# A decoder layer on one core: row sums and the residual's scale and shift move to VectorE beside the index search, and the search is spread over more products

## The chip, the cores and the metric

The kernel runs on one core of a Trainium2 chip. A core has five engines, each with its own queue of instructions that it works through in order: TensorE (PE; its weight loads are listed as PEld), VectorE (DVE), ScalarE (ACT), GpSimd (POOL) and SyncE (SP), which here only issues DMA transfers. They wait for each other through semaphores. The metric is the device time of one execution in microseconds (us), the median of several runs.

## The reference

The reference computes one decoder layer for 512 tokens of width 1024, in float32. Cut to what matters here:

```python
h = layer_norm(x, ln_emb_g, ln_emb_b)
q_att, c_kv, q_idx, k_idx, w_idx, cv_b, cv_c, cv_x, g_att, g_conv = split(h @ w_in)
score = sum over 8 heads of relu(q_idx . k_idx / 8) * w_idx        # 512 x 512, causal
sel   = the 128 best keys of each query's row
att   = softmax(q . k over sel) . values                            # 8 heads, latent rank 128
conv_y = cv_b * causal_dwconv3(cv_c * cv_x)
merged = sigmoid(g_att + b0) * (att @ w_br_att) + sigmoid(g_conv + b1) * (conv_y @ w_br_conv)
h = layer_norm(ALPHA * h + merged @ w_o, ln1_g, ln1_b)              # ALPHA = 2 ** 0.25
# then a gated MLP with a causal width-3 convolution, an embedding term and a last layer_norm
```

## The kernel before

Everything is kept in float32 accuracy by splitting each operand of a product into a high part and a low part (the rest): a product is three matmuls, high by high, high by low and low by high (L157 to L159). For each chunk of weights (128x1024 numbers) SP loads the raw numbers (wr), ACT casts the high part (wh, L76), and DVE or POOL subtracts to get the low part (wl, L143). A letter of the chunk, "v" or "p", says which of the two.

The program is a list of steps, one or two chunks each, and each engine's queue simply gets its instructions in the order in which the code is written: nothing reorders them. `plan()` builds the steps. Ahead of step i come the casts and low parts of chunks some steps ahead (`advance`, with a lead of 3 steps and 4 raw buffers), then the functions that are entered for that step in `preps`, then the step itself. The order of the steps is: the index queries (q_idx) with the scores between them, two early products of the convolution, then from `at_first` on conv block 0's b, the four attention queries (qa, split by POOL), the c, x and b products of conv blocks 1 to 3, then gates (gt, and gtb by blocks), branches (br), the output product (wo) and the MLP.

Three streams of side work stand between these steps.

- **The index search.** For each of three blocks of 128 queries (over 256, 384 and 512 keys), 16 rounds on DVE find the best eight scores of each row (MAX8, L596) and strike them out (MATCH_REPLACE8, L598). A last operation (madd, L601) makes the mask. The scores themselves are summed on DVE (L586). The search is a generator: behind each step, the run loop takes rounds until their summed costs, an estimate that the generator gives for each, pass a budget, SIDE_NS. Each round is put down at 2.084 times the number of keys plus 395, in ns: 928, 1195 and 1462.
- **The attention.** Its steps are tied to later steps of the list (ATT_AT). One step sends the logits (lg) through a reduction on DVE with the mask (L671), exponentials on ACT (L675), a reciprocal and the scaling on DVE (L677, L679); a later one transposes the rows on PE (pT, L687). A step that needs a mask which is not ready takes the rest of that block's rounds first. The third block of queries (384 keys) is the first to go in two halves.
- **The conv blocks.** For each, DVE multiplies c and x (cvu, L764), ACT and POOL apply the three taps (cvt, L750 to L755), DVE multiplies by b (cvy, L771), and ACT and POOL split the result (cvT, L773 and L774).

The residual: x's normalized rows (`xb`, before the embedding norm's scale and shift) are spilled to DRAM at the end of `start()`, loaded again as `hr` when memory is free, and multiplied by ALPHA times the scale (ge) and shifted by ALPHA times the shift (be) there (L1028, L1029), ahead of the last branches. ACT makes the two ALPHA products (L1024), and `onto` puts the rows into the accumulators of wo (L1047).

The row sums: four sums and differences of blocks of the transposed h (`hx` in the trace, `first_sum`, L795), needed for the gates by blocks, run on POOL in the four steps from `at_first` − 1 on; their splits (fsh, fsl) come nine steps later and more.

Of the kernel before, what the change touches and what calls it, by code (L numbers as in the profile page):

```python
# [11 lines left out]
OP = mybir.AluOpType  # L12
# [3 lines left out]
D = 1024  # L16
NB = S // P
# [7 lines left out]
ALPHA = 2.0 ** 0.25  # L25
# [60 lines left out]
class Kern:  # L86
# [1 line left out]
    WHL = 4  # L88
    LEAD = 3
    NK4 = 28  # L90
    SIDE_NS = 3600
    ATT_AT = (-2, 0, 3, 5, 7, 9, 12, 14)

    def __init__(self, ctx, tc, a, out):
# [60 lines left out]
    def mm3(self, out, wh, wl, xh, xl, start, stop):  # L155
        t = self.nc.tensor
        t.matmul(out, wh, xh, start=start, stop=False)  # L157
        t.matmul(out, wh, xl, start=False, stop=False)  # L158
        t.matmul(out, wl, xh, start=False, stop=stop)  # L159
# [105 lines left out]
    def start(self):  # L265
        nc, a = self.nc, self.a
# [217 lines left out]
        rest = small_norm((2, 3))  # L484
        self.advance(0, 5)
        rest()
        for b in range(NB):
            nc.sync.dma_start(self.hdram[b], self.xb[b])
        for i in range(3):
            nc.sync.dma_start(self.pwdram[i], pw[i].rearrange("p b n -> p (b n)"))  # L490

# [20 lines left out]
    def plan(self):  # L512
        nc, a = self.nc, self.a
# [276 lines left out]
        def first_sum(n):  # L790

            b11, b12, b21, b22 = (self.hblock[g, h] for g in range(2) for h in range(2))
            to, x, y, op = ((b11, b11, b12, OP.subtract), (b12, b22, b12, OP.subtract),
                            (b22, b11, b22, OP.add), (b21, b22, b21, OP.subtract))[n]
            return lambda: nc.gpsimd.tensor_tensor(to, x, y, op=op)  # L795

        def first_parts(n):
            def f():
# [10 lines left out]
        def block_mm(o, w, at, rows, start, stop):  # L809
            wh, wl = (t.rearrange("p (k m) -> p k m", k=KC)[:, 4 * at:4 * at + 4] for t in (w.hi, w.lo))  # L810
            for c, (xh, xl) in enumerate(rows):
                for i, (l, r) in enumerate(((wh, xh), (wh, xl), (wl, xh))):
                    nc.tensor.matmul(o, l[:, c], r, start=start and c + i == 0, stop=stop and c == 3 and i == 2,  # L813
                                     skip_group_check=True)
# [147 lines left out]
        at_first = len(self.steps)  # L962
# [7 lines left out]
        at_slot, pairs = [], {}  # L970
# [29 lines left out]
        for n in range(4):  # L1000
            self.preps.setdefault(at_first - 1 + n, []).append(lambda n=n: first_sum(n)())
            self.preps.setdefault(at_first + (9, 11, 12, 13)[n], []).append(first_parts(n))
# [4 lines left out]

        def res_load():

            ge, be = self.k4("ge"), self.k4("be")  # L1010
            self.bcast("ln_emb_g", D, ge, nc.sync)
            self.bcast("ln_emb_b", D, be, nc.sync)
            self.res_affine = ge, be

        def res_rows():
            self.hr = []
# [2 lines left out]
                nc.sync.dma_start(t, self.hdram[b])  # L1019
                self.hr.append(t)  # L1020

        def res_scale():
            for t in self.res_affine:
                nc.scalar.mul(t, t, ALPHA)  # L1024

        def res_affine(b):
            t, (ge, be) = self.hr[b], self.res_affine
            nc.vector.tensor_tensor(t, t, ge, op=OP.mult)  # L1028
            nc.vector.tensor_tensor(t, t, be, op=OP.add)  # L1029

        def ln1_load():
            self.g1, self.b1 = self.k4("g1"), self.k4("b1")
            self.bcast("ln1_g", D, self.g1)
            self.bcast("ln1_b", D, self.b1)

        self.preps.setdefault(at_slot[15], []).append(res_load)
        self.preps.setdefault(at_slot[17], []).append(res_rows)
        self.preps.setdefault(at_slot[19], []).append(res_scale)
        for b in range(NB):
            self.preps.setdefault(at_slot[20 + b // 2], []).append(lambda b=b: res_affine(b))  # L1040

        self.zps = {}

# [423 lines left out]
        for n, (name, i) in enumerate(copies):  # L1467
            at = at_ple - 2 + n // 2 if n < 4 else at_ple + 1 + (n - 4) * 4 // 5 if n < 20 else at_ple + 16 + 3 * (n - 20)
# [224 lines left out]
    def run(self):  # L1693
        for i, fn in enumerate(self.steps):
# [5 lines left out]
            if self.side_from is not None and i >= self.side_from:  # L1700
                left = self.SIDE_NS
                while left > 0:
# [93 lines left out]
```

## Time and profile before

| | before |
|---|---|
| median of 3 runs | 745.28 us (745.15 to 746.37) |
| the profiled execution | 745.23 us |
| its span, first to last instruction | 743.5 us |
| around the span | 1.7 us |
| mean granted clock of PE | 0.991 |
| busy: PE, DVE, ACT, POOL | 725.6, 615.6, 425.6, 269.2 us |

A time at the head of a row of the timeline is counted from the start of the span; the second number is the duration, and a bracket at the end holds the idle time ahead of the row and what ended it. In a row of waits stand the sum, the number of times and the longest. In a group's row stand the busy time and the mean duration in ns of one. Where the first index block ends and so on is told by the shapes: 128x256, 128x384 and 128x512 rows are the search over 256, 384 and 512 keys.

### The profile page before, as it was taken

To read this page: it belongs to the slowest core of one execution; us is meant where nothing else is said; L and a number is where in the kernel's file an instruction comes from. 1 tells how busy PE (TensorE), PEld (TensorE's weight loads), DVE (VectorE), ACT (ScalarE), POOL (GpSimd) and SP (SyncE) were. 2 spreads that over 40 slices of the span, in tenths; PEclk is the share of its full clock that TensorE was granted. 3 is DMA by queue.
4 is the path that set the end of the run, shared out by engine and by line. 5 is a ranking of instruction groups with operands and counts; after the bars stand their busy time and mean duration, and the time that the engine had idled before them with its cause. 6 is when DMAs were issued, how large, how long until landed. Compare 5 with 4: busy or idle time off the path is not lost.

```text
span 743.5 us, 12196 instructions
## 1 busy us (share of the span) xinstructions
PE 725.6 (98%) x4399; PEld 640.4 (86%) x4399; DVE 615.6 (83%) x1045; ACT 425.6 (57%) x718; POOL 269.2 (36%) x332
## 2 busy tenths in 40 slices
PE   9999899999999999799999999999999999999995
PEld 5998678888879998588888999999999998888885
DVE  5867999975557657889898899999999889987797
ACT  5645434468766554343565666777667665665630
POOL 4304698765755821320101233443332212211002
PEclk9999999999999999899999999999999999999999
DMA  9473379759999999195998999899989878999661
GB/s 354 109 274 100 102 255 370 267 185 271 233 218 184 224 274 395 42 314 203 299 393 250 323 276 253 223 250 250 236 233 254 235 216 212 273 256 278 224 212 57
DMA packets 61867, 178.02 MB, mean 239 GB/s; under 512 B 7232, under 2 KB 7360, under 8 KB 61424
## 3 DMA queue, kind: packets, MB, share of 16 engines
q1 hardware_dynamic: 43968, 140.56, 53.8%
q0 software_dynamic: 16976, 35.27, 26.8%
q10 hardware_dynamic: 864, 1.43, 0.6%
q8 instruction: 34, 0.56, 0.3%
q14 instruction: 25, 0.20, 0.1%
HBM read 171.46 MB, written 70.78 MB: 326 GB/s over the span
## 4 chain that ended last, share of the span: by engine, by line
PE 88%; DVE 6%; ACT 2%; POOL 1%; DMA 1%; issue 1%; DVEq 0%; ACTq 0%; POOLq 0%
PE ffb L813 23%; PE gtb L813 5%; PE dn L1527 5%; PE dn L1526 5%; PE dn L1528 5%; PE cv L157 2%; PE cv L159 2%; PE cv L158 2%; PE gt L157 2%; PE wo L918 2%; PE wo L917 2%; PE gt L159 2%; PE gt L158 2%; PE wo L916 2%; PE pg L1168 2%; PE pg L1169 2%
## 5 line engine op out<-in xcount | busy, mean ns | idle before, releaser
L143 DVE TENSOR_TENSOR wl<-wr,wh 128x1024 fp32r<-128x1024 f32 (+1 forms) x175 | 199.8, 1157 | 45.9 <-ACT wh L76 44.5
L76 ACT CAST wh<-wr 128x1024 fp32r<-128x1024 f32 (+1 forms) x186 | 180.5, 978 | 73.3 <-PE dn L1528 15.7
L1453 POOL TENSOR_TENSOR behind<-token,neghalf 128x1 f32<-128x1 f32 x112 | 82.3, 857 | 241.4 <-ACT token L1452 205.2
L813 PE MATMUL ffb<-hsh,wh 128*128 128x256 f32 x304 | 86.1, 283 | 0.0
L813 PE MATMUL ffb<-hsl,wh 128*128 128x256 f32 x304 | 86.0, 283 | 0.0
L813 PE MATMUL ffb<-hsh,wl 128*128 128x256 f32 x304 | 86.0, 283 | 0.0
L813 PE MATMUL ffb<-h1T,wh 128*128 128x256 f32 x456 | 83.9, 283 | 0.1
L813 PEld LDWEIGHTS ffb<-h1T,wh 128*128 128x128 f32 x456 | 71.1, 192 | 0.4 <-ACT c L1368 0.3
L813 PE MATMUL ffb<-h1T,wl 128*128 128x256 f32 x228 | 64.7, 284 | 0.2 <-DVE wl L143 0.2
L813 PEld LDWEIGHTS ffb<-hsl,wh 128*128 128x128 f32 x304 | 58.4, 192 | 0.0
L813 PEld LDWEIGHTS ffb<-hsh,wh 128*128 128x128 f32 x304 | 58.4, 192 | 0.0
L813 PEld LDWEIGHTS ffb<-hsh,wl 128*128 128x128 f32 x304 | 58.4, 192 | 0.0
L143 POOL TENSOR_TENSOR wl<-wr,wh 128x1024 fp32r<-128x1024 f32 x15 | 36.0, 2406 | 27.5 <-ACT wh L76 27.5
L813 PEld LDWEIGHTS ffb<-h1T,wl 128*128 128x128 f32 x228 | 43.7, 192 | 0.4 <-DVE wl L143 0.4
L185 POOL TENSOR_TENSOR rstd<-veps,neghalf 128x1 f32<-128x1 f32 x12 | 8.0, 666 | 99.3 <-DVE nm L208 65.2
L1329 POOL DMA_DIRECT2D ws<-ws x38 | 39.3, 1170 | 11.2 <-issue 6.1
L1329 POOL DMA_DIRECT2D ws<-in_w_a x38 | 36.2, 1363 | 6.1 <-issue 3.9
L159 PE MATMUL cv<-hT,wl 128*128 128x512 f32 x80 | 31.3, 391 | 0.4 <-POOL wl L143 0.4
L157 PE MATMUL cv<-hT,wh 128*128 128x512 f32 x80 | 31.4, 392 | 0.0
L158 PE MATMUL cv<-hT,wh 128*128 128x512 f32 x80 | 31.1, 389 | 0.0
L743 DVE SCALAR_TENSOR_TENSOR ff<-c,vec,ff 128x510 f32<-128x510 f32 x38 | 28.5, 750 | 1.3
L740 ACT ACTIVATE ff<-c,vec 128x512 f32<-128x512 f32 x38 | 29.3, 811 | 0.4 <-DVE c L1374 0.2
(363 smaller groups left out, 2087.8 us busy)
## 6 DMA issues: line engine op xcount, KB each, us to landing
wr<-in_w_a SPq DMA_DIRECT2D x61, 512.0 KB, 4.5
ws<-in_w_a SPq DMA_DIRECT2D x76, 256.0 KB, 6.1
wr<-ws SPq DMA_DIRECT2D x38, 512.0 KB, 6.4
ws<-in_w_a POOLq DMA_DIRECT2D x38, 256.0 KB, 8.6
ws<-ws POOLq DMA_DIRECT2D x38, 256.0 KB, 11.0
wr<-in_w_b SPq DMA_DIRECT2D x15, 512.0 KB, 6.0
wr<-in_w_dn SPq DMA_DIRECT2D x15, 512.0 KB, 6.6
wr<-in_w_a SPq DMA_DIRECT2D x19, 256.0 KB, 6.9
```

The source lines that it names most:

```text
L76: nc.scalar.copy(hi, raw)
L143: (self.nc.vector if eng == "v" else self.nc.gpsimd).tensor_tensor(lo, raw, hi.bitcast(F32), op=OP.subtract)
L157: t.matmul(out, wh, xh, start=start, stop=False)
L158: t.matmul(out, wh, xl, start=False, stop=False)
L159: t.matmul(out, wl, xh, start=False, stop=stop)
L740: nc.scalar.activation(dst, src, AF.Identity, bias=v[:, bcol:bcol + 1], scale=v[:, wcol + 2 * tap:wcol + 2 * tap + 1])
L813: nc.tensor.matmul(o, l[:, c], r, start=start and c + i == 0, stop=stop and c == 3 and i == 2, skip_group_check=True)
L1329: return lambda: nc.gpsimd.dma_start(to, what, accum_op=OP.add, max_dma_last_dim=4096)
L1453: nc.gpsimd.tensor_tensor(self.sm("behind", [P, 1], bufs=2), t, self.neghalf, op=OP.mult)
L1526: nc.tensor.matmul(o, ah, wh[:, i, c], start=first, stop=False, skip_group_check=free)
L1527: nc.tensor.matmul(o, ah, wl[:, i, c], start=False, stop=False, skip_group_check=free)
L1528: nc.tensor.matmul(o, al, wh[:, i, c], start=False, stop=last, skip_group_check=free)
```

## The change

Five things are edited; the products on PE and their order stay the same.

- The four `hx` operations of 128x1024 run on DVE in place of POOL, in the same steps.
- ge and be are loaded at step 2 in place of a late step, and ACT multiplies them by ALPHA one step behind `at_first`.
- The scale and shift (two operations of 128x1024 for each of four blocks of rows) act on x's rows, in the eight steps from `at_first` + 3 on, still on DVE, and no longer on the loaded `hr` rows.
- The spills of x's rows to DRAM follow there, each behind its block's two operations; the loads back stay where they were.
- SIDE_NS is 2800 in place of 3600, so fewer rounds of the search follow a step (three of 256 or 384 keys give 2784 and 3585, two of 512 give 2924).

```diff
-    SIDE_NS = 3600
+    SIDE_NS = 2800
...
-        for b in range(NB):
-            nc.sync.dma_start(self.hdram[b], self.xb[b])
...
-            return lambda: nc.gpsimd.tensor_tensor(to, x, y, op=op)
+            return lambda: nc.vector.tensor_tensor(to, x, y, op=op)
...
+        def res_scale():
+            for t in self.res:
+                nc.scalar.mul(t, t, ALPHA)
+
+        def res_affine(b, i):
+            x = self.xb[b]
+            return lambda: nc.vector.tensor_tensor(x, x, self.res[i], op=(OP.mult, OP.add)[i])
+
+        def res_spill(b):
+            return lambda: nc.sync.dma_start(self.hdram[b], self.xb[b])
...
-        def res_affine(b):
-            t, (ge, be) = self.hr[b], self.res_affine
-            nc.vector.tensor_tensor(t, t, ge, op=OP.mult)
-            nc.vector.tensor_tensor(t, t, be, op=OP.add)
...
-        self.preps.setdefault(at_slot[15], []).append(res_load)
-        self.preps.setdefault(at_slot[17], []).append(res_rows)
-        self.preps.setdefault(at_slot[19], []).append(res_scale)
+        for at, f in ((2, res_load), (at_first + 1, res_scale), (at_slot[17], res_rows)):
+            self.preps.setdefault(at, []).append(f)
         for b in range(NB):
-            self.preps.setdefault(at_slot[20 + b // 2], []).append(lambda b=b: res_affine(b))
+            for i in range(2):
+                self.preps.setdefault(at_first + 3 + 2 * b + i, []).append(res_affine(b, i))
+            self.preps.setdefault(at_first + 6 + 2 * b, []).append(res_spill(b))
```

The line numbers of the changed kernel are smaller by two from L490 on: L764 is L762 there, L671 is L669.

First place, DVE's queue around conv block 2, some steps ahead of the first attention reductions. Before (a MAX and a MATCH_REPLACE are one round; tk are the search's rows):

```order
L764 TENSOR_TENSOR cvu_1548<-cv_1523,cvc_1470 128x512
L596 MAX m_358_1558<-tk_0_1427 128x8
L598 MATCH_REPLACE tk_1_1428<-m_358_1558,tk_0_1427 128x512
L596 MAX m_359_1561<-tk_1_1428 128x8
L598 MATCH_REPLACE tk_0_1427<-m_359_1561,tk_1_1428 128x512
L596 MAX m_360_1564<-tk_0_1427 128x8
L598 MATCH_REPLACE tk_1_1428<-m_360_1564,tk_0_1427 128x512
L771 TENSOR_TENSOR cvy_1602<-cv_1577,cvt_1550 128x512
```

The same place in the change, with the last block of x's rows (x_74):

```order
L1018 TENSOR_TENSOR x_74<-x_74,ge 128x1024
L762 TENSOR_TENSOR cvu_1547<-cv_1522,cvc_1468 128x512
L594 MAX m_354_1557<-tk_0_1502 128x8
L596 MATCH_REPLACE tk_1_1503<-m_354_1557,tk_0_1502 128x512
L594 MAX m_355_1560<-tk_1_1503 128x8
L596 MATCH_REPLACE tk_0_1502<-m_355_1560,tk_1_1503 128x512
L1018 TENSOR_TENSOR x_74<-x_74,be 128x1024
L769 TENSOR_TENSOR cvy_1600<-cv_1575,cvt_1549 128x512
```

A step holds two rounds in place of three and one operation on x's rows more. Counted up to the first reductions, the search over 512 keys has 14 rounds there before and 7 in the change; the 32 rounds over 256 and 384 keys stand ahead of them in both.

Second place, DVE's queue between the scaling of the second attention step's rows (p_1) and the reductions of the third. Before:

```order
L679 TENSOR_SCALAR p_1_1888<-p_1_1888,rs_1887 128x256 x4
L679 TENSOR_SCALAR p_1_1889<-p_1_1889,rs_1887 128x256 x4
L143 TENSOR_TENSOR wl_1945<-wr_1571,wh_1944 128x1024
L143 TENSOR_TENSOR wl_1976<-wr_1642,wh_1975 128x1024
L1450 MEMSET token_1981 128x1
```

In the change:

```order
L677 TENSOR_SCALAR p_1_1887<-p_1_1887,rs_1885 128x256 x4
L143 TENSOR_TENSOR wl_1943<-wr_1567,wh_1942 128x1024
L594 MAX m_397_1973<-tk_0_1502 128x8
L596 MATCH_REPLACE tk_1_1503<-m_397_1973,tk_0_1502 128x512
L594 MAX m_398_1976<-tk_1_1503 128x8
L596 MATCH_REPLACE tk_0_1502<-m_398_1976,tk_1_1503 128x512
L143 TENSOR_TENSOR wl_1980<-wr_1637,wh_1979 128x1024
```

Two rounds follow each low part (wl) there; five rounds and the madd stand between these rows and the third reductions, where none stood before. Four more stand between the first attention step's scaling and the second reductions, where two and the madd stood.

Third place, DVE's queue in the last branches, between two low parts. Before:

```order
L143 TENSOR_TENSOR wl_3513<-wr_3364,wh_3512 128x1024
L1028 TENSOR_TENSOR hr_3297<-hr_3297,ge 128x1024
L1029 TENSOR_TENSOR hr_3297<-hr_3297,be 128x1024
L1028 TENSOR_TENSOR hr_3299<-hr_3299,ge 128x1024
L1029 TENSOR_TENSOR hr_3299<-hr_3299,be 128x1024
L902 TENSOR_TENSOR sig_2740<-br_3522,sig_2740 128x512
```

In the change:

```order
L143 TENSOR_TENSOR wl_3517<-wr_3374,wh_3516 128x1024
L900 TENSOR_TENSOR sig_2754<-br_3522,sig_2754 128x512
L902 TENSOR_TENSOR sig_2754<-sig_2754 128x512
L900 TENSOR_TENSOR sig_2914<-br_3540,sig_2914 128x512
L902 TENSOR_TENSOR sig_2914<-sig_2914 128x512
```

The operations on the loaded rows are gone; the gate's products (sig) follow the low part at once. The same holds one low part earlier, for the first two blocks of rows.

More of the change, by code (lines that the diff above doesn't have):

```diff
@@ L1008, in res_load @@
         def res_load():
[L1010 to L1013, printed above, removed]
+            self.res = self.k4("ge"), self.k4("be")
+            for name, t in zip(("ln_emb_g", "ln_emb_b"), self.res):
+                self.bcast(name, D, t, nc.sync)
+        def res_scale():
[6 more added lines that the diff above has]
+            return lambda: nc.sync.dma_start(self.hdram[b], self.xb[b])
         def res_rows():
@@ L1020, in res_rows @@
                 self.hr.append(t)
-        def res_scale():
-            for t in self.res_affine:
-                nc.scalar.mul(t, t, ALPHA)
-        def res_affine(b):
-            t, (ge, be) = self.hr[b], self.res_affine
-            nc.vector.tensor_tensor(t, t, ge, op=OP.mult)
-            nc.vector.tensor_tensor(t, t, be, op=OP.add)
         def ln1_load():
```

## The prediction

> **What bounds the kernel now.** I read the page first, then the waits of TensorE, then a table of stages, then single stretches of the timeline.
>
> ```profile
> PE 725.6 (98%) x4399; PEld 640.4 (86%) x4399; DVE 615.6 (83%) x1045; ACT 425.6 (57%) x718; POOL 269.2 (36%) x332
> PE 88%; DVE 6%; ACT 2%; POOL 1%; DMA 1%; issue 1%; DVEq 0%; ACTq 0%; POOLq 0%
> PE br L157 <- DVE sig L902: 4.7, 1, 4.7
> PE qa L159 <- POOL wl L143: 2.0, 1, 2.0
> ```
>
> TensorE (PE) is busy for 98% of the span and carries 88% of the chain of waits; its products are the same in both kernels. So only two things can change the time: the few stalls that it has now, and new ones. Of the present ones two matter: 4.7 us for VectorE (DVE) late, in the branches, and 2.0 us for a low part from POOL, early. The second question is where PE is nearly late. The stages tell; the columns are window, PE, PEld, DVE, ACT and POOL busy, the granted clock of PE, the DMA share and GB/s:
>
> ```profile
> 80.00:100.00 20.00, 17.70 (x70) 13.86 (x69) 18.72 (x52) 9.03 (x15) 13.79 (x7) 0.91 0.59 193
> 100.00:120.00 20.00, 19.56 (x87) 15.88 (x86) 18.97 (x49) 5.36 (x7) 18.42 (x12) 1.00 0.87 294
> 120.00:140.00 20.00, 20.00 (x90) 16.57 (x89) 19.31 (x40) 11.35 (x18) 14.90 (x9) 1.00 0.85 315
> 300.00:320.00 20.00, 15.27 (x59) 12.15 (x58) 16.37 (x18) 7.43 (x12) 6.54 (x5) 0.83 0.24 79
> ```
>
> From 80 to 140 us DVE is as full as PE (56.99 of 60 us), since the index search runs there; at 300 it is full again, for another reason. DVE's 83% over the whole span hides both places.
>
> **The removed part: the late stall.** The residual's rows go through four multiplies and four adds:
>
> ```profile
> L1028 DVE TENSOR_TENSOR hr<-hr,ge x4: 1212/1216/1219, 293.0 to 306.3; 128x1024 f32<-128x1024 f32 x4
> L1029 DVE TENSOR_TENSOR hr<-hr,be x4: 1224/1224/1225, 294.2 to 307.6; 128x1024 f32<-128x1024 f32 x4
> 303.92 1.21 DVE L1028 TENSOR_TENSOR hr<-hr,ge 128x1024 f32<-128x1024 f32 x1
> 308.71 0.68 DVE L902 TENSOR_TENSOR sig<-br,sig 128x512 f32<-128x512 f32 x1
> 309.54 0.76 PE L157 MATMUL br<-at,wh 128*128 128x512 f32 x1 [4.73 <-DVE sig L902]
> 313.51 0.51 PE L157 MATMUL br<-at,wh 128*128 128x512 f32 x1
> ```
>
> The last four stand right ahead of the gate's product (sig) that frees PE's accumulator. Without them it starts at 303.92 in place of 308.71 and ends at 304.60; PE wanted it at 309.54 − 4.73 = 304.81. So the whole 4.73 goes, with 0.2 to spare. Behind the stall PE runs at half clock: nine products from 309.54 to 313.51 take 3.97 us, and at the step of 0.22 us that the pair 88.17, 88.39 below shows they would take 1.98. That is another 2.0. **Gain: 6.7 us**; bounds 4.7 (if PE finds another reason to be slow) and 6.7. Nothing else is late next there: the low part behind these rows is then earlier.
>
> **The part that stays: the early stall.** Four combinations of blocks (hx) leave POOL, and it looks as if they made POOL's low part late. They don't:
>
> ```profile
> 88.17 0.39 PE L158 MATMUL qa<-hT,wh 128*128 128x512 f32 x1
> 88.39 0.39 PE L159 MATMUL qa<-hT,wl 128*128 128x512 f32 x1
> 91.82 0.77 PE L159 MATMUL qa<-hT,wl 128*128 128x512 f32 x1 [2.00 <-POOL wl L143]
> 86.75 0.68 DVE L771 TENSOR_TENSOR cvy<-cv,cvt 128x512 f32<-128x512 f32 x1
> 88.16 1.29 POOL L774 TENSOR_TENSOR cvT<-cvy,cvT 128x512 fp32r<-128x512 f32 x1 [6.21 <-ACT cvT L773]
> 89.40 2.37 POOL L143 TENSOR_TENSOR wl<-wr,wh 128x1024 fp32r<-128x1024 f32 x1
> ```
>
> POOL was through with its hx at 81.95 and then idle for 6.21 us, for a copy that waits for DVE's cvy, which stands behind four search rounds and the score sums. In the change an hx stands ahead of cvy too (+1.2), and the scores lose the hx on POOL that slowed them (below: −1.1). I cost this stall at no change; bounds −1.1 and +1.2.
>
> **The added part on DVE.** Twelve operations of 128x1024 come to it ahead of the first attention step: four hx and eight on x's rows. By the rows of the removed ones, of the same shape and engine, one takes 1.22 us. To make room, the search is thinned: 7 of its 14 rounds over 512 keys move behind the first attention reductions. A round is one MAX8, one load and one MATCH_REPLACE8:
>
> ```profile
> L596 DVE MAX8 m<-tk 128x8 f32<-128x512 f32 x13 | 9.0, 692 | 0.3
> L598 DVE MATCH_REPLACE8 tk<-m,tk 128x512 f32<-128x512 f32 x13 | 8.8, 676 | 0.0
> 139.23 0.70 DVE L596 MAX8 m<-tk 128x8 f32<-128x512 f32 x1
> 140.75 0.69 DVE L596 MAX8 m<-tk 128x8 f32<-128x512 f32 x1
> 74.11 8.71 DVE L586 SCALAR_TENSOR_TENSOR score<-rl,widx,score 128x512 f32<-128x512 f32 x6 [2.65 <-ACT rl L584]
> 146.70 0.28 DVE L671 CUSTOM_DVE_ANT_0 p<-lg,madd 128x128 f32<-128x128 f32 x1
> 152.23 3.82 DVE L679 TENSOR_SCALAR p<-p,rs 128x128 f32<-128x128 f32 x8
> 155.43 1.03 PE L687 MATMUL pT<-ident,p 128*128 128x128 f32 x8
> ```
>
> From MAX8 to MAX8 a round is 1.52 us. One hx lands ahead of cvu of the first conv block, before 2.65 us in which DVE waits anyway, so it is free. The sum up to the first reductions: 11 × 1.22 − 7 × 1.52 = 13.4 − 10.6 = +2.8, less 1.1 for the scores: six of them take 8.71 beside a low part and an hx of POOL, and some half of the hx's 2.4 is theirs. **+1.7 us**. There is no cover for it: DVE's table rows are full, the reductions at 146.70 follow the search with no idle time before them, and the last scaling ends at 156.05 while PE's transposes of the same rows run from 155.43, head by head, to 156.46. PE is 0.1 us at most behind DVE there.
>
> That sum has each operation alone. But DVE and POOL do not run two such operations side by side:
>
> ```profile
> 68.55 2.31 DVE L143 TENSOR_TENSOR wl<-wr,wh 128x1024 fp32r<-128x1024 f32 x1
> 68.29 1.49 POOL L624 TENSOR_TENSOR w_uk<-w_uk_raw,w_uk 128x512 fp32r<-128x512 f32 x1 [3.70 <-ACT w_uk L623]
> 185.79 1.21 DVE L143 TENSOR_TENSOR wl<-wr,wh 128x1024 fp32r<-128x1024 f32 x1
> L795 POOL TENSOR_TENSOR hx<-hx,hx x4: 2382/2502/2713, 62.0 to 97.7; 128x1024 f32<-128x1024 f32 x4
> ```
>
> The same low part takes 1.21 us alone and 2.31 where POOL's operation runs until 69.78: 1.23 of waiting and 1.08 of work. MAX8 and MATCH_REPLACE8, which the moved rounds are made of, show no such growth: their 692 and 676 ns are means over windows in which POOL was working. So the exchange puts operations that wait in the place of some that don't. The bounds: nothing, if every one falls into a gap of POOL; 2.4 us each, POOL's longest operation, if every one meets its start. POOL is busy for 33.3 of the 40 us from 100 to 140, so 0.83 of the eight x operations meet something, and half of 2.4 is left on average: 8 × 0.83 × 1.2 = 8.0. For the hx behind the scores POOL is emptier (13.8 of 20, of which 7.5 were the hx): 3 × 0.32 × 1.2 = 1.2. Two that stand back to back share one wait, so I take 7.5 rather than 9.2; the whole range is 0 to 13. **First transposes late by 1.7 + 7.5 − 0.1 = 9.1 us.** Part of this already shows ahead of it: ACT's conv taps wait for cvu, the casts of weights stand behind them on ACT, and PE waits for those.
>
> The Trainium skill says the same more sharply ("SBUF — State Buffer", section "Who interferes with whom"): VectorE and GpSimd share a port pair under an exclusive lock, and the loser is blocked until the other is done. The 2.31 us row agrees. By that rule the sum is the 9.1 above; without it 1.6.
>
> **The seven moved rounds.** They come back behind the first step: 9 rounds and a madd stand ahead of the third reductions where 2 and a madd stood, so DVE gets 7 × 1.52 = 10.6 us more there.
>
> ```profile
> 175.16 1.23 DVE L143 TENSOR_TENSOR wl<-wr,wh 128x1024 fp32r<-128x1024 f32 x1 [0.66 <-ACT wh L76]
> 177.47 0.06 DVE L1450 MEMSET token<- 128x1 f32 x1 [0.91 <-POOL behind L1453]
> 179.40 0.55 DVE L671 CUSTOM_DVE_ANT_0 p<-lg,madd 128x384 f32<-128x384 f32 x1 [0.90 <-issue]
> 169.76 0.20 DVE L677 RECIPROCAL rs<-sums 128x8 f32<-128x8 f32 x1 [4.11 <-ACT p L675]
> 184.39 1.48 DVE L679 TENSOR_SCALAR p<-p,rs 128x384 f32<-128x384 f32 x4
> 188.61 0.60 PE L687 MATMUL pT<-ident,p 128*128 128x128 f32 x4
> ```
>
> DVE's idle time in between is 0.66 + 0.91 + 0.92 (a second wait like that one) + 0.90 = 3.4 us that the rounds can use. The 4.11 ahead of the reciprocals they can't: these wait for exponentials, which wait for reductions that are themselves later, and no round is put between. So the third reductions are late by 10.6 − 3.4 = 7.2. The scaling's four parts end at 185.87, and PE takes the first two at 188.61: a slack of 3.4, counting the half that it needs first. **New stall: 7.2 − 3.4 = 3.8 us**, bounds 0 and 7, and 2.0 behind it at half clock, as at 309. (In a stretch that DVE sets, a half clock before the last stall lies inside DVE's lateness, so it counts once.)
>
> **The rest** costs nothing that I can find. ge and be are scaled on ACT early in place of late, two operations; ACT is busy for 9.03 and 5.36 of the 20 us there, and if they were not covered they would cost 2.1:
>
> ```profile
> L1024 ACT ACTIVATE ge<-ge x1: 1053/1053/1053, 284.2 to 284.2; 128x1024 f32<-128x1024 f32 x1
> L488 SPq DMA_DIRECT2D hsp<-x x4: 424/863/1336, 40.4 to 42.7; - x4
> ```
>
> The four spills leave SP's queue at 40 us and go behind the adds, at 100 to 150, where the DMA engines are busy for 0.85 to 0.87. Behind a waiting spill the weight loads of the next steps wait in the same queue. Those already wait there for buffers that POOL's low parts free, and they run three steps ahead; bounds 0 and 3, I take 0. Nobody reads the spilled rows before 273.
>
> **Sum:** +9.1 + 3.8 + 2.0 − 6.7 = +8.2. The profiled execution takes 745.23 us, 0.05 from the median of 745.28: **753.4 us**.
>
> **The rivals**, with 0.2% (1.5 us) as what a measurement tells from no change:
>
> (1) The forecast: DVE's extra waits decide. 0.58; its own range 748 to 758.
>
> (2) No waiting between DVE and POOL. The bare sum: 1.6 + 3.8 + 2.0 − 6.7 = +0.7, so 745.9. For it: POOL loses 10.1 us of hx, which makes gaps. Against: its taps and low parts remain, and the table above has 18.42 of 20 busy. 0.09.
>
> (3) The intended outcome, faster: the late stall goes and the early stretch holds. One mechanism decides it: whether DVE reaches the first reductions no later than now, that is, whether the twelve operations cost less than the seven rounds. It would need them at 0.9 us each or to start earlier, and the third step's 7.2 to shrink under its slack of 3.4. Then 745.2 − 6.7 = 738.5. For it: one hx is free, the scores run faster, and PE's early stall lets everything of PE's wait with it. Against: a row of 1.22 and 0.1 us of slack. From a lateness of 5 us in all it is no gain any more. 0.19.
>
> (4) Every one of the eleven meets POOL, and POOL's own low parts come late because it waits for DVE in turn: 13 in place of 7.5, so 758.9. For it: 18.42 of 20. Against: DVE's waits shift it into POOL's gaps. 0.14.
>
> Faster 0.19 (3, nothing of the others); within 0.2% 0.10 (2, and the low edge of 1); slower 0.71. The range, 741 to 759, leaves out the larger part of (3) and the upper half of (4).
>
> **What would show it.** In the changed profile PE's waits lose "br <- DVE sig" at 309; the window 300:320 has the clock near 1.00. PE gets waits for p or weights between 110 and 200, some 13 us in all, and PE's busy share there falls. The x operations take 1.2 alone, and 2 to 3 where a POOL operation runs. The first transposes stand near 164. Wrong is the price of the waits if their mean is under 1.5 us; wrong is the third step if PE does not wait at its transposes; wrong is all of it if the first transposes stand at 157 or earlier.

## The result

| | before | after |
|---|---|---|
| median | 745.21 us (745.02 to 746.37, 4 runs) | 750.54 us (749.82 to 751.16, 4 runs) |
| the profiled execution | 745.23 us | 751.16 us |
| its span | 743.5 us | 749.4 us |

The change makes the kernel slower: the ratio is 1.0068, 95% interval 1.005 to 1.0085, which is +5.3 us between the medians. The forecast was slower, 753.4 us, with a range of 741 to 759.

The profile after, read in the same order as before. First the waits of TensorE (PE): sum, times, longest.

```profile
PE pT L685 <- DVE p L677: 4.4, 3, 2.0
PE cv L159 <- POOL wl L143: 3.5, 1, 3.5
PE cv L157 <- DVE cvy L769: 1.8, 1, 1.8
PE lg L166 <- ACT pT L691: 0.9, 1, 0.9
PE qa L159 <- POOL wl L143: 0.7, 1, 0.7
```

The 4.7 us for sig is gone, and so is most of the early 2.0 us (0.7 is left). In their place PE waits for rows of the attention (p, and pT, the transposed copy), for a low part of POOL and for an accumulator that cvy frees, 10.6 us in the first four rows. The table of stages has the place (PE, PEld, VectorE (DVE), ACT and POOL busy, granted clock, DMA share, GB/s):

```profile
80.00:100.00 20.00, 19.26 (x85) 15.67 (x84) 19.00 (x50) 11.76 (x17) 13.58 (x7) 1.00 0.71 220
100.00:120.00 20.00, 20.00 (x90) 16.56 (x89) 19.02 (x34) 1.54 (x2) 10.98 (x6) 1.00 0.96 330
120.00:140.00 20.00, 16.36 (x64) 12.75 (x63) 19.55 (x35) 8.87 (x13) 14.96 (x7) 0.91 0.55 186
140.00:160.00 20.00, 17.23 (x93) 13.82 (x91) 15.29 (x42) 12.52 (x30) 13.98 (x7) 1.00 0.80 264
160.00:180.00 20.00, 17.70 (x89) 14.75 (x90) 15.39 (x44) 10.07 (x26) 13.37 (x13) 0.91 0.87 274
300.00:320.00 20.00, 20.00 (x90) 16.57 (x89) 13.84 (x16) 9.18 (x14) 8.58 (x6) 1.00 0.52 192
```

At 300 us PE is full and at full clock. From 120 to 180 it loses 8.7 of 60 us, and the clock drops twice. DVE stays as full as it was to 140 us (57.57 of 60).

Since PE runs the same 4399 products in both, the n-th of one can be set against the n-th of the other. The difference of their starts is PE's lateness:

| at | before | after | lateness |
|---|---|---|---|
| end of the early stretch | 105.06 | 100.97 | -4.1 |
| behind the low part's wait | 130.12 | 130.42 | +0.3 |
| behind the wait for cvy | 144.39 | 147.89 | +3.5 |
| behind the first transposes | 158.02 | 166.74 | +8.7 |
| behind the third transposes | 190.82 | 203.26 | +12.4 |
| behind the place of the late stall | 313.09 | 319.01 | +5.9 |

A gain of 4.1 early, a loss of 12.8 up to the first transposes, 3.7 more at the third, and a gain of 6.5 to 7.0 late. Behind that it stays between 5.4 and 6.9 us.

DVE's groups from the last six score sums to the first reductions show where its time went (the first of the four hx stands ahead of them). Before (74 to 146.6 us; busy time, mean ns of one, idle time ahead):

```profile
L586 DVE SCALAR_TENSOR_TENSOR score<-rl,widx,score 128x512 f32<-128x512 f32 (+2 forms) x6 | 8.4, 1425 | 3.0 <-ACT rl L584 2.6
L601 DVE TENSOR_SCALAR madd<-tk 128x256 f32<-128x256 f32 (+1 forms) x2 | 2.3, 1152 | 0.1
```

After (73 to 153.6 us):

```profile
L1018 DVE TENSOR_TENSOR x<-x,be 128x1024 f32<-128x1024 f32 x4 | 8.1, 2036 | 0.0
L584 DVE SCALAR_TENSOR_TENSOR score<-rl,widx,score 128x512 f32<-128x512 f32 (+2 forms) x6 | 6.2, 1066 | 3.0 <-ACT rl L582 2.7
L1018 DVE TENSOR_TENSOR x<-x,ge 128x1024 f32<-128x1024 f32 x4 | 6.1, 1524 | 0.0
L793 DVE TENSOR_TENSOR hx<-hx,hx 128x1024 f32<-128x1024 f32 x3 | 5.1, 1693 | 0.0
L599 DVE TENSOR_SCALAR madd<-tk 128x256 f32<-128x256 f32 (+1 forms) x2 | 3.8, 1889 | 0.0
```

Eleven operations of 1.22 us would be 13.4; they took 8.1 + 6.1 + 5.1 = 19.3. That is 5.9 of waiting, where the forecast took 7.5; the two madd, which it left out, have 1.5 more, so 7.4 in all. Single rows show the partner: the longest one starts at 109.08, while POOL's pair of low parts runs, and ends 1.08 us behind that pair (106.22 + 4.76 = 110.98; 109.08 + 2.98 = 112.06). So it waited for 1.90 us and then worked, as the row of 2.31 us in the prediction did. The other row is an operation that met nothing.

```profile
106.22 4.76 POOL L143 TENSOR_TENSOR wl<-wr,wh 128x1024 fp32r<-128x1024 f32 x2
109.08 2.98 DVE L1018 TENSOR_TENSOR x<-x,be 128x1024 f32<-128x1024 f32 x1
115.61 1.22 DVE L1018 TENSOR_TENSOR x<-x,ge 128x1024 f32<-128x1024 f32 x1
```

### The profile page after: what moved, and what is told of

Its sections match the earlier page's. It is cut to its first block, busy times and chain, and to the rows that moved or that the text cites. A ratio compares the mean times of both kernels' runs of the same rounds, so it can differ in the third digit from the quotient of the medians.

```text
span 749.4 us, 12203 instructions
## 1 busy us (share of the span) xinstructions
PE 728.0 (97%) x4399; PEld 641.3 (86%) x4399; DVE 620.6 (83%) x1049; ACT 425.5 (57%) x718; POOL 267.7 (36%) x328
## 4 chain that ended last, share of the span: by engine, by line
PE 68%; DVE 18%; DMA 5%; issue 3%; ACT 3%; POOL 1%; SPq 1%; DVEq 0%; POOLq 0%; ACTq 0%
PE ffb L811 15%; PE gtb L811 5%; PE dn L1528 5%; PE dn L1526 5%; PE dn L1527 5%; DVE wl L143 4%; DMA wr<-ws 3%; DVE tk L596 3%; DVE m L594 2%; PE wo L916 2%; PE wo L914 2%; PE wo L915 2%; DVE score L584 2%; PE br L157 2%; PE pg L1169 2%
## 5 line engine op out<-in xcount | busy, mean ns | idle before, releaser
L1453 POOL TENSOR_TENSOR behind<-token,neghalf 128x1 f32<-128x1 f32 x112 | 89.5, 934 | 251.6 <-ACT token L1452 204.8
L143 POOL TENSOR_TENSOR wl<-wr,wh 128x1024 fp32r<-128x1024 f32 x15 | 38.7, 2586 | 24.0 <-ACT wh L76 24.0
L1329 POOL DMA_DIRECT2D ws<-in_w_a x38 | 37.7, 1464 | 3.4 <-issue 2.5
## 6 DMA issues: line engine op xcount, KB each, us to landing
ws<-ws POOLq DMA_DIRECT2D x38, 256.0 KB, 10.6
```

Of the source, the lines that this page charges most:

```text
L143: (self.nc.vector if eng == "v" else self.nc.gpsimd).tensor_tensor(lo, raw, hi.bitcast(F32), op=OP.subtract)
L1329: return lambda: nc.gpsimd.dma_start(to, what, accum_op=OP.add, max_dma_last_dim=4096)
L1453: nc.gpsimd.tensor_tensor(self.sm("behind", [P, 1], bufs=2), t, self.neghalf, op=OP.mult)
```

## The experiments

Theory: DVE sets the end of the early stretch, and waits beside POOL are a good part of what it lost. Rivals: the length of the operations alone, the thinned search, or the early stall counting in full. All times beside an experiment are from its own chip: before took 744.3 to 744.9 us there, so ratios compare best.

**The x operations without waits.** The eight operations on x's rows become one-operand MAX8 over the same rows; the residual is left unscaled.

```diff
-            return lambda: nc.vector.tensor_tensor(x, x, self.res[i], op=(OP.mult, OP.add)[i])
+            return lambda: nc.vector.max(self.sm("m8", [P, 8], bufs=2), x)
```

> The changed kernel, with the eight operations on x's rows replaced by MAX8 over the same 128x1024 rows (the residual is left unscaled and unshifted). MAX8 reads one operand and, by the 692 ns row of 512 columns, takes about 1.36 us in place of 1.22 alone. Theory of waits beside POOL: the x rows' 14.7 us (9.8 alone and 4.9 of waiting) become some 10.9, DVE reaches the first reductions 3.5 to 4 us earlier than in the changed kernel, at about 149.8, and the time falls to 746 to 747.5. Rival, that the operations' own length decides and not the waits: 8 x 0.14 = 1.1 us more, 751 to 752.

744.68 us, ratio to before 1.0002 (0.9991 to 1.0013): some 5 us less than the changed kernel. The group of eight:

```profile
L1018 DVE MAX8 m<-x 128x8 f32<-128x1024 f32 x8 | 9.7, 1218 | 0.0
```

and the first reductions, of the changed kernel and of this one:

```profile
153.69 0.28 DVE L669 CUSTOM_DVE_ANT_0 p<-lg,madd 128x128 f32<-128x128 f32 x1
```

```profile
148.61 0.28 DVE L669 CUSTOM_DVE_ANT_0 p<-lg,madd 128x128 f32<-128x128 f32 x1
```

One MAX8 takes 1.218 us (I had put it at 1.36), as long as the operation that it replaces takes alone, and all eight are within 3 ns of each other. So DVE's queue, the count and the length are the same; only the waits are gone, and the first reductions come 5.1 us earlier. The waits are shown as the cause of that part, and the rival of 751 falls. The madd, which still meets POOL, kept its own.

The waits that went were on both engines. In the changed kernel POOL's operations stretch too where they meet an x operation, such as the one that runs from 125.73 to 127.27; the same low part, in the changed kernel and in this one:

```profile
126.15 3.33 POOL L143 TENSOR_TENSOR wl<-wr,wh 128x1024 fp32r<-128x1024 f32 x1
```

```profile
123.38 2.40 POOL L143 TENSOR_TENSOR wl<-wr,wh 128x1024 fp32r<-128x1024 f32 x1
```

It ends 3.7 us later in the changed kernel, 2.8 of that by a later start and 0.9 by its own waiting, and PE's wait of 3.5 us for it is 0.2 here. The forecast's sum had charged the waits to DVE alone; that POOL waits in turn stood only in the rival of 758.9.

**The search's budget.** SIDE_NS back to 3600 in the changed kernel, and 2800 alone in the kernel before.

```diff
-    SIDE_NS = 2800
+    SIDE_NS = 3600
```

> The changed kernel with SIDE_NS back at 3600, so 14 rounds of 512 stand ahead of the first reductions again. Theory, that DVE's load ahead of the first reductions decides: 7 rounds of 1.52 come back there, the first reductions are 10.6 us later than the changed kernel's (at about 164), the stall at the third step's transposes goes (3.7 us), so 756 to 758. Rival, that thinning the search is what costs: about 745 to 747.

758.1 us, ratio 1.0187 (1.0164 to 1.021). The first reductions stand at 166.65, 13.0 us later than in the changed kernel: seven rounds, and more waits of the x operations. Over 256 keys a step holds four rounds with both budgets, since three of 928 ns do not pass 2800; what the smaller budget thins is the search over 384 keys (three in place of four) and over 512 (two in place of three).

> The kernel before with only SIDE_NS 2800. Theory: the first reductions can start no earlier than their logits (about 2.2 us earlier than before, at 144.5), which gains nothing, since PE stands at its own work; the third reductions are late by 10.6 - 3.4 - 2.2 = 5 us against a slack of 3.4, so a stall of 0 to 2 us and up to 2 at half clock: 745 to 749. Rival, that the seven rounds behind the first step cost their full stall as in the changed kernel (3.8 and 2.0): 751.

747.75 us, ratio 1.0046 (1.003 to 1.0063). The first reductions start at 144.68, no longer behind the search but behind 3.06 us of idle time; the transposes of the third step wait for 1.1 us and the logits behind them for 0.9, and PE is 3.4 us late behind them. Thinning costs 3.4 us by itself, and saves 8.9 (1.0187 - 1.0068, of 745) where DVE is too full: it is what kept this change from being worse.

**The parts alone.** The hx back on POOL in the changed kernel; the hx alone, and the residual's part alone, in the kernel before.

```diff
-            return lambda: nc.vector.tensor_tensor(to, x, y, op=op)
+            return lambda: nc.gpsimd.tensor_tensor(to, x, y, op=op)
```

> The changed kernel with the four hx back on POOL. Theory, that PE's end is set by DVE at the first and third steps: DVE loses 4.8 us of hx and gains 3.0 of slower and later scores, so it is 1.8 us earlier at best; POOL has 10 us more and the waits of the x operations grow by 0 to 3; the early stall of PE comes back (2 us and half clock) but lies inside DVE's lateness: 748.5 to 752. Rival, that the early stall counts in full: 754 to 755.

748.19 us, ratio 1.0049 (1.0032 to 1.0066). PE's early wait is back:

```profile
PE qa L159 <- POOL wl L143: 2.0, 1, 2.0
```

Yet the time is no longer than the changed kernel's. So that wait does not count where DVE is late behind it. In the profiled execution no half clock follows the wait (the granted clock from 80 to 100 us is 1.00, where it was 0.91 before), so it tests the 2.0 us alone.

> The kernel before with only the four hx moved to DVE. Theory, that DVE sets the first transposes: three hx of 1.22 and about 1.2 us of waits come to DVE, the scores give back 3.0 (they start 0.9 earlier and take 2.15 less), so the first reductions are about 1.9 late; PE's early stall shrinks by 4 us and is waited out there, with 1 to 2 us at half clock: 746.5 to 748.5. Rival, that a freer POOL is worth the whole early stall: 741.

748.17 us, ratio 1.0042 (1.0025 to 1.0059). PE is 3.9 us early at 101 us and 3.1 late behind the first transposes. The waits in this kernel:

```profile
PE pT L687 <- DVE p L679: 4.9, 2, 3.2
PE br L157 <- DVE sig L902: 4.7, 1, 4.7
PE qa L159 <- POOL wl L143: 0.8, 1, 0.8
```

The early wait is smaller, and the transposes take it back with interest.

> The kernel before with only the residual's part: loads, scale, shift and spills early, on x's rows; hx on POOL and SIDE_NS 3600. Theory: DVE gets eight operations, 9.8 us alone and 5 to 7 of waits beside POOL, with nothing taken away ahead of the first reductions: these are 15 to 17 us late; the late stall of PE goes (6.7): 754 to 757. Rival, that the rows fit into gaps and the gain of the late stall stays: 738.5 to 742.

755.45 us, ratio 1.0147 (1.0122 to 1.0172). The first reductions are 17.2 us late (163.9 for 146.7), the late stall goes. Both theories' numbers were apart by 12 us, and DVE's load is the one that holds. The three parts alone cost 3.1, 10.9 and 3.4 us, 17 in sum, and 5 together.

**Ways to the gain of the late stall.** The residual's operations on the loaded rows stay, spread over four steps from one step earlier (with their loads and the scaling of ge and be).

```diff
-        self.preps.setdefault(at_slot[17], []).append(res_rows)
+        self.preps.setdefault(at_slot[16], []).append(res_rows)
...
-            self.preps.setdefault(at_slot[20 + b // 2], []).append(lambda b=b: res_affine(b))
+            self.preps.setdefault(at_slot[19 + b], []).append(lambda b=b: res_affine(b))
```

> The kernel before with the residual's operations on the loaded rows left on DVE, but one block of rows per step from one step earlier (four steps), in place of two blocks in each of two steps; the three loads and the scaling come one step earlier too. Theory, that the late stall is only DVE's queue in one step: the 4.7 us and the 2.0 at half clock behind it go, and nothing early changes: 738.5 to 740. Rival, that DVE is full over that whole stretch, or that the loaded rows come too late: the stall turns up at another product, 742 to 746.

744.34 us, ratio 0.9996 (0.9985 to 1.0007): the theory missed. The stall is still 4.4 us. A likely reason is in ACT's queue: the first branch's cast waits longer for its weights, which now land behind the rows.

```profile
281.63 1.05 ACT L76 CAST wh<-wr 128x1024 fp32r<-128x1024 f32 x1 [5.46 <-DMA wr<-in_w_br]
```

The same cast stood at 278.77 before, with a wait of 2.58 for its weights. The low part, and with it DVE's whole queue, starts 2.9 us later there. How much of the stall this explains was not tried apart.

**The search one step later.** The first four rounds no longer stand ahead of cvy.

```diff
-        self.side_from = at_first - 1
+        self.side_from = at_first
```

> The kernel before with the search's first four rounds one step later, so that cvy of the first conv block no longer stands behind them on DVE (the hx stay on POOL); three rounds of 512 move behind the first reductions. Theory: cvy comes 3.9 us earlier, PE's early stall (2.3 and about 1.9 at half clock) goes, DVE reaches the first reductions 4.5 us earlier and so does not give it back: 740.5 to 742.5. Rival, that the low part behind it waits for POOL's hx all the same, or that DVE takes it back at the first or third transposes: 744 to 746.

748.63 us, ratio 1.0053 (1.0018 to 1.0088): missed. The nine executions of this kernel fall into two groups, five from 746.84 to 748.63 us and four from 756.48 to 759.57; 748.63 is the median of all nine, and the ratio counts the 756.48 in. The median of the five is 746.94, 2.0 us above that of the kernel before on its chip (744.94), so the theory misses by that too. The profile is of the upper group. In it PE gains 4.0 us early, as expected, and then a madd of 256 columns takes 11.65 us:

```profile
99.08 11.65 DVE L601 TENSOR_SCALAR madd<-tk 128x256 f32<-128x256 f32 x1
```

```profile
98.63 2.39 POOL L143 TENSOR_TENSOR wl<-wr,wh 128x1024 fp32r<-128x1024 f32 x1
100.97 1.30 POOL L153 TENSOR_TENSOR qa<-qac,qa 128x512 fp32r<-128x512 f32 x1
102.22 2.40 POOL L143 TENSOR_TENSOR wl<-wr,wh 128x1024 fp32r<-128x1024 f32 x1
104.58 1.29 POOL L153 TENSOR_TENSOR qa<-qac,qa 128x512 fp32r<-128x512 f32 x1
105.83 4.75 POOL L143 TENSOR_TENSOR wl<-wr,wh 128x1024 fp32r<-128x1024 f32 x2
```

It starts behind POOL's first of six operations and ends 0.15 us behind the last (110.58). Why the lower group doesn't gain stays open, since no profile shows it.

**POOL's idle time ahead of the search.** POOL idles from 39 to 60 us before. In one kernel it gets the four multiplies of x's rows there, at the end of the start (the adds go on DVE in steps 1 and 2, SIDE_NS 3600); in one the four hx; in one both.

```diff
+        for f in self.res_early[2]:
+            f()
...
+            self.preps.setdefault(1 + min(b, 1), []).append(res_affine(b, 1))
+            self.preps.setdefault(3, []).append(res_spill(b))
```

> The kernel before (SIDE_NS 3600, hx on POOL late), with the residual's part done ahead of the search: ge and be are loaded during the start, the four multiplies of x's rows run on POOL in its idle time from 39 to 59 us, the four adds on DVE among its gaps from 43 to 51 us, and the spills follow. Theory, that it is the place beside the full search that costs and not the move as such: DVE reaches the first reductions within 1 us of before, the late stall goes (4.7 and 2.0): 738.5 to 740. Rival, that waits beside POOL in 39 to 59 us delay the scores, whose lateness is kept up to the first transposes: 742 to 746.

```diff
-            self.preps.setdefault(at_first - 1 + n, []).append(lambda n=n: first_sum(n)())
+            self.preps.setdefault(0, []).append(lambda n=n: first_sum(n)())
```

> The kernel before, with the four hx still on POOL but in the first step, in POOL's idle time from 39 to 59 us. Theory: the scores behind 57 us lose the two hx beside them (some 3 us, as they did when hx went to DVE), DVE reaches the first reductions about 3 us earlier, PE's early stall shrinks by up to 4 us, and the first transposes come 2 to 3.5 us earlier: 741.5 to 743.5. Rival, that the hx now wait with DVE's operations from 42 to 50 us and the gain is lost there: 744.5 to 746.

> Both: the residual's part as in d1 and the hx in the first step, eight operations on POOL from 39 us on, the hx last. Theory: the gains add, less 1 to 2 us since the hx now run beside the first scores (49 to 59 us): 735.5 to 738.5. Rival, that POOL's queue of eight (19 us) makes its next low part and the scores late: 740 or more.

745.94, 748.53 and 750.32 us; ratios 1.0016 (1.0005 to 1.0028), 1.005 (1.0036 to 1.0064) and 1.0067 (1.0043 to 1.0092). All three missed the theory, and the reason that all three show is a wait of PE for the keys' rows (ckT) of 5.4, 5.8 and 12.0 us. POOL and then DVE, in the kernel with the multiplies:

```profile
39.26 9.84 POOL L1022 TENSOR_TENSOR x<-x,ge 128x1024 f32<-128x1024 f32 x4
39.81 2.43 DVE L400 SCALAR_TENSOR_TENSOR kn<-cks,kmv,kig 128x64 f32<-128x64 f32 x1
42.34 4.54 DVE L403 SCALAR_TENSOR_TENSOR kn<-kn,krstd,kib 128x64 f32<-128x64 f32 x2
46.81 2.44 DVE L406 SCALAR_TENSOR_TENSOR cn<-cks,krstd,kvg 128x128 f32<-128x128 f32 x1
49.17 0.28 DVE L400 SCALAR_TENSOR_TENSOR kn<-cks,kmv,kig 128x64 f32<-128x64 f32 x1
```

The last row is the same operation as the second, when POOL has just ended its four (39.26 + 9.84 = 49.10). Each small operation of DVE waits out one of POOL's; PE waits 5.4 us for the keys' rows behind them, and is 7.8 us late by 113 us. The late stall goes in the first and the third kernel, which gives 6.6 back. In the second PE's lateness falls from 8.8 us to 3.5 by 110 us, so the gain of the theory is there, but smaller than the loss ahead of it. POOL's idle time was not free, because DVE had short two-operand work there.

**DVE's own idle time, and half of the work.** Two of the four blocks of rows are scaled and shifted on DVE in two long gaps ahead of the search, where POOL is idle or nearly so (the first behind the keys' low parts, the second behind the first cvu); the other two stay late, one per step; the row loads stay where they were.

```diff
+            x = self.xb[b]
+            for i in range(2):
+                nc.vector.tensor_tensor(x, x, self.res[i], op=(OP.mult, OP.add)[i])
...
+            step(and_scores(2 + i, both(w.second) if i else w.second), [w])
...
-        for b in range(NB):
-            self.preps.setdefault(at_slot[20 + b // 2], []).append(lambda b=b: res_affine(b))
+        for b in (2, 3):
+            self.preps.setdefault(at_slot[(20, 22)[b - 2]], []).append(lambda b=b: res_affine(b))
+        self.preps.setdefault(2, []).append(lambda: early_rows(0))
```

> The kernel before (SIDE_NS 3600, hx on POOL), with the residual's part of two of the four blocks of rows done early, on DVE alone and only where it is idle: the first block's two operations in the 2.85 us behind the keys' low parts (46.7 to 49.5), the second's in the 2.65 us behind the first cvu (71.5 to 74.1). The other two blocks stay late, one per step (the first where two stood, the second two steps on); the row loads stay where they were. Theory: 4.9 us of operations go in DVE's idle time at no cost and with no POOL beside them, the first transposes stay within 0.5 us, the late queue loses 4.9 or more, so its stall of 4.7 and the 2.0 at half clock go: 738.5 to 740.5. Rival, that the late stretch is bound by the loop of DVE and ACT in each branch step, so the stall only moves to the output product: 742 to 745.

739.24 us (737.68 to 740.43), ratio 0.9925 (0.9911 to 0.9938): faster than both kernels. The two gaps and what fills them:

```profile
46.64 1.22 DVE L942 TENSOR_TENSOR x<-x,ge 128x1024 f32<-128x1024 f32 x1
47.89 1.23 DVE L942 TENSOR_TENSOR x<-x,be 128x1024 f32<-128x1024 f32 x1
49.47 0.56 DVE L147 TENSOR_TENSOR qi<-qi,qi 128x384 fp32r<-128x384 f32 x1 [0.35 <-ACT qi L146]
71.13 1.21 DVE L942 TENSOR_TENSOR x<-x,ge 128x1024 f32<-128x1024 f32 x1
72.37 1.23 DVE L942 TENSOR_TENSOR x<-x,be 128x1024 f32<-128x1024 f32 x1
73.86 2.93 DVE L591 SCALAR_TENSOR_TENSOR score<-rl,widx,score 128x512 f32<-128x512 f32 x2 [0.26 <-ACT rl L589]
72.81 3.44 POOL L760 TENSOR_TENSOR cvt<-cvt,tap 128x511 f32<-128x511 f32 x2 [3.29 <-ACT tap L759]
```

Each operation takes its 1.21 to 1.23 us alone, and what follows still waits for ACT. The last of them is met by POOL's cvt (the last row), and there it is POOL that waits: its two take 3.44 us, where they took 2.79 before. PE is 0.8 us late at 107 us, has no wait for sig in the branches, and is 6.1 us early behind the place of the late stall.

## Why the prediction was right, point by point

**The late stall** (forecast: 4.73 and 2.0 gone, 6.7): right. PE's lateness falls by 6.5 in the rows of the table, and by 7.0 until 477 us. Nothing else was late there.

**The early stall** (forecast: no change, bounds -1.1 to +1.2): wrong. PE gained 4.1 us: 1.9 from an earlier low part, 1.6 from the half clock that did not follow its wait, and 0.6 from a later short wait that went. I had charged cvy with the hx in front of it and given the scores back 1.1; they began 0.9 us earlier and took 2.2 less (8.4 to 6.2), so cvy came at 84.84 in place of 86.75.

```profile
73.23 6.56 DVE L584 SCALAR_TENSOR_TENSOR score<-rl,widx,score 128x512 f32<-128x512 f32 x6 [2.65 <-ACT rl L582]
84.84 0.69 DVE L769 TENSOR_TENSOR cvy<-cv,cvt 128x512 f32<-128x512 f32 x1
```

The score sum that stood beside the second hx takes 2.62 us before and 0.47 in the change: it had waited out nearly a whole hx, and not half of one. The time didn't show the gain: DVE was late behind it, and the kernel with the hx back on POOL is no slower.

**The sum up to the first reductions** (forecast for the transposes: +1.7 alone, +7.5 of waits, 9.1): right in mechanism, 2 us too high. Measured: 153.69 for 146.70, +7.0, and +7.6 at the scaling. The terms close: 13.4 for eleven operations alone, less 10.6 for seven rounds, 7.4 of waits, less 3.1 for the scores, 7.1 in all. The scores gave 3.1 in place of 1.1, and that is the term that was mis-sized: from one row of 8.71 us for six I had guessed half of one hx, and the single operations would have shown more. That the waits came near my 7.5 is in part luck: the eleven waited 5.9, and the 1.5 of the two madd were not in the sum. My range for the waits, 0 to 13, also does not fit the bound that I named: eleven times 2.4 is 26, and 13 is half of it.

By the Trainium skill ("SBUF — State Buffer", section "Who interferes with whom") VectorE and GpSimd have a port pair that one of them holds for a whole instruction. With the eight x operations as one-operand MAX8 the first reductions come 5.1 us earlier, in line with that rule; the 11.65 us of one madd is longer than any one instruction of POOL, so there the wait covered several.

**Where it would show** (forecast: some 13 us of waits, for p or weights, from 110 to 200 us): right; it is 10.6 us. The first transposes were put near 164; they run from 160.25 to 163.95, in two pieces with waits of 1.2 and 2.1 us, the first piece 4.8 and the second 7.3 us later than before.

```profile
160.25 0.83 PE L685 MATMUL pT<-ident,p 128*128 128x128 f32 x4 [1.22 <-DVE p L677]
163.13 0.82 PE L685 MATMUL pT<-ident,p 128*128 128x128 f32 x4 [2.05 <-DVE p L677]
```

**The moved rounds** (forecast: third reductions 7.2 us later still, a stall of 3.8 and 2.0 at half clock): the lateness is right, 193.53 for 179.40, that is 14.1, or 7.1 beyond the 7.0. PE's own lateness grew by 3.7. The 2.0 at half clock did not come: PE's waits there are 1.2 and 0.9 us, and the granted clock is 1.00 from 167 to 210 us. The drops of clock stand behind the 3.5 us at 129 and behind the first transposes, at 164.

```profile
193.53 0.55 DVE L669 CUSTOM_DVE_ANT_0 p<-lg,madd 128x384 f32<-128x384 f32 x1
129.54 0.66 PE L159 MATMUL cv<-hT,wl 128*128 128x512 f32 x1 [3.55 <-POOL wl L143]
130.00 0.63 PE L157 MATMUL cv<-hT,wh 128*128 128x512 f32 x1
133.52 0.40 PE L157 MATMUL cv<-hT,wh 128*128 128x512 f32 x1
```

**The sum**: +8.2 forecast, +5.3 measured between the medians. The two profiled spans differ by 5.9, which is the table's +8.7, +3.7 and −6.5 beside the forecast's +9.1, +3.8 and 2.0, and −6.7. That 8.7 is close to 9.1 is luck: DVE brought the second piece of the transposes only 7.3 us late, and some 1.5 us of half clock behind it, which I had not counted, made up most of the difference. The 2.0 at half clock behind the third step is the other term that did not come.

**The rivals.** No waiting (745.9): refuted by the MAX8 kernel, which shows what the change is without the waits of the x operations, 744.7 (ratio 1.0002). The intended outcome (738.5): its late gain is real and came in full, and the last kernel takes most of it by going where DVE is idle. All eleven meeting POOL (758.9): the waits of single x operations go from none to 1.8 us, so not every one; its other half, that POOL waits for DVE in turn, did happen.

## What to carry to other kernels

Work that moves from an engine's full stretch to another full stretch is not hidden because TensorE looks like the bound; look at what stands with no idle time ahead of the first row that TensorE waits for. Price an operation with two SBUF operands on VectorE by what GpSimd runs beside it, and prefer gaps of VectorE in which GpSimd is idle too: there four operations cost under 1 us, and beside a busy GpSimd eight cost 4.5 us more than their length. Short operations suffer most, because each waits out a whole operation of the other.

## What the runs showed of the hardware

An operation of 0.28 us took 2.43 us beside back-to-back 2.4 us operations of GpSimd, one of its own for one of GpSimd's. A madd of 256 columns (0.43 us for 512 alone) waited through six of them, 11.65 us, in the profiled execution of one kernel. MAX8 over 1024 columns took 1.216 to 1.219 us in the same places where two-operand operations took up to 2.98. The waiting went both ways: a low part of 2.40 us on GpSimd took 3.33 beside an x operation. What decides whether VectorE gets in between two operations of GpSimd was not settled.

The same early wait of TensorE, 2.0 us, was followed by a stretch at half clock in the profiled executions of four kernels (the granted clock from 80 to 100 us is 0.91 in the kernel before, in the one with the budget alone and in the one with the residual's part alone, and 0.83 in the last one) and by none in those of two others (1.00, in the one with the hx back on POOL and in the one with the rows spread). So in these traces the length of a wait does not tell alone whether a half clock follows.
